# Three small steps of a gate computation moved from VectorE to ScalarE in a streaming encoder kernel

## The chip, the cores and the metric

The kernel runs on one core of one Trainium2 chip. A core has a matrix engine (TensorE, PE in the profile, with its weight loads as PEld), a vector engine (VectorE, DVE), an activation engine (ScalarE, ACT), a third engine for element work (GpSimd, POOL), and an engine that here only issues DMAs (SyncE, SP). Each engine runs its own list of instructions strictly in the order in which the program holds them, and waits at an instruction until the semaphores it needs have been raised by the others. The metric is the device time of one execution, in microseconds; the kernel before took 1362.77 us (median of 3 runs, 1361.56 to 1366.36).

## The reference

One step of an encoder layer over 1024 prompt frames and 32 frames of a running stream. Three groups of heads mix over time in parallel (gated linear attention, HGRN2, mLSTM), and a gated feed-forward network follows. The change lies in the gates of the mixing step:

```python
log_a = log_sigmoid(gg @ gla_w_gate + gla_b_gate) / 16          # first group, tiles 0 and half of 3
log_f = log(lbh + (1 - lbh) * sigmoid(fr))                      # second group, tiles 1, 2, half of 3
k     = (1 - lbh) * sigmoid(-fr)
...
b = cumsum(log_a or log_f)                                      # per block of 64 frames
...
ig = mi + b_i;  log_fm = log_sigmoid(mf + b_f)                  # third group, five rows
w  = exp(b_i - b_j + ig_j - m_i)
```

`lbh` is a lower bound for the gate, one number per channel. `(1 - lbh) * sigmoid(-fr)` can be computed as `exp(log sigmoid(-fr)) * (1 - lbh)`, or as one `exp(log sigmoid(-fr) + log(1 - lbh))`.

## The kernel before, in words

The 1056 frames are taken in three groups (`GROUPS`, L27): 384, 384, and 256 prompt frames with the 32 running ones, 288 columns. For each group `inproj` (L357) computes the normalised input times `w_in`. Every product is a sum of three matmuls (`mm3`, L100: high times high, low times high, high times low), and every weight tile comes in by DMA, is cast on ScalarE or VectorE to its high part and has its low part formed by a subtraction on GpSimd or VectorE (`split`, L105). In group 0 the low parts of the tiles that the gates need are formed on GpSimd and written out, so that groups 1 and 2 load them.

The feature tiles come in a fixed order: 8, 6, 7, 3, 2, 0, 4, 5, 1, 10, 11, 12, 13. In the profile their weights are `wf_8` to `wf_13` and their PSUM results `pf`. All these results, and those of the token tiles (`pv`, weights `wt_1` to `wt_7`), share three PSUM banks of the pool `psb` (tag `big`); TensorE can begin a tile only when the one three places earlier has been read.

Between the tiles stands the work on the gates:

- `decay(f, fill)` (L513), for f = 0 to 3, brings the gate's argument to `fr` and computes `exp(-|fr|)` into `e`, and for f = 1 to 3 the term with the lower bound.
- `rows()` (L564) does the same for the five rows of the third group, on five partitions. `er` is the last of the eight parts of the tile `e`. The exponential at L631 is its first step on ScalarE.
- `logs()` (L524) takes the logarithm of all eight parts in one instruction.
- `decays(f, ins)` (L528) forms the logarithm of the sigmoid (L533), its counterpart for the key (L535), the exponential of that (L536), the product with 1 - lower bound (`oml`, L537), adds the term with the lower bound (L538), divides by 16 where the first group's rows lie (L541, f = 0 and 3; the column of `vecs` holds 1/16 or 1 by partition), and runs the sum over the block (L542). `out_units` writes keys and sums to DRAM by SP.
- `conv(j, ps)` (L374) is a short convolution for tiles 8 and 10 to 13: a copy out of PSUM (L378), a scaled copy (L390), three multiply-adds on VectorE (L392), a tanh (L395, recorded at L113), a last product (L396).

While group g is projected, the mixers of the group before run beside it: `mixer` (L728) is a generator, and `merge` (L1694) advances it a few steps after each tile. A mixer works in three pairs of levels. A pair's scores are matmuls into the one PSUM tile `sc` (L858, a single buffer); VectorE copies them into `P` under a mask (L813, `COPY_PREDICATED`), and the next pair's scores can begin only when the pair before has been copied.

What order the instructions have on each engine is not written out: `schedule_with_timeline_sim` (L81) lets the Tile scheduler place them by its own estimate of their times, within the dependencies, priorities (`high_priority`) and `issue_after` marks of the code. A changed step can so move its neighbours. ScalarE evaluates its functions from a table that is loaded by an own instruction, `ACT_TABLE_LOAD`; the build places one ahead of any function that the loaded table does not hold. The table of the first load serves exponential, tanh, square and copies; the logarithm at L526 has another.

Of the kernel before, what the change touches and what calls it, by code (L numbers as in the profile page):

```python
# [12 lines left out]
AF = mybir.ActivationFunctionType  # L13
ALU = mybir.AluOpType
# [77 lines left out]
def body(ctx: ExitStack, tc: tile.TileContext, a: dict):  # L92
    nc = tc.nc
    act, dve, pool, pe, sp = nc.scalar, nc.vector, nc.gpsimd, nc.tensor, nc.sync
# [62 lines left out]
    def const(name, shape, dt=F32, src=None):  # L157
        t = cp.tile(shape, dt, name=name)
        if src is not None:
            sp.dma_start(t, src)  # L160
        return t
# [10 lines left out]
    vecs = const("vecs_sb", [128, 12], F32, a["vecs"])  # L172
# [41 lines left out]
    dve.tensor_tensor(lb, lsm, lsm, op=ALU.subtract)  # L214
    oml = const("oml", [128, 4])
    dve.tensor_scalar(oml, lb, -1.0, 1.0, op0=ALU.mult, op1=ALU.add)

    def rstd_of(out, ss, n, cols, width, eps=EPS):

        pool.tensor_scalar(out, ss, 1.0 / width, eps, op0=ALU.mult, op1=ALU.add)  # L220
        pool.tensor_tensor(out, out, mhalf[:n, :cols], op=ALU.pow)
# [124 lines left out]
    def out_units(g, dst, dst_s, rng, src, smp_off=None, rows=slice(0, 128), drows=None):  # L346

        t0, pl, sl = GROUPS[g]
        u0, nu = t0 // 128, pl // 128
        drows = rows if drows is None else drows  # L350
        sp.dma_start(dst[(slice(u0, u0 + nu), drows) + rng].rearrange("u p n -> p u n"),
                     src[rows, :pl].rearrange("p (u n) -> p u n", n=128))
        if sl:
            so = pl if smp_off is None else smp_off
            sp.dma_start(dst_s[(drows,) + rng], src[rows, so:so + sl])

    def inproj(g, xh, xl, normed, scaled=None):  # L357
        t0, pl, sl = GROUPS[g]
        T = pl + sl
        R = slice(96, 101)  # L360

        def t1(tag, bufs=1, w=T, dt=F32):
            return pf.tile([128, w], dt, tag=tag, name=f"{tag}_{g}", bufs=bufs)
# [133 lines left out]
        ig = t1("r_ig")  # L497
# [30 lines left out]
        def decays(f, ins):  # L528

            with tc.issue_after(ins.ins):  # L530
                fr, ls = fr4[:, f], e4[:, f]
                lo = (128, 0, 0, 64)[f]
                dve.scalar_tensor_tensor(ls, fr, 0.0, ls, op0=ALU.min, op1=ALU.subtract)  # L533
                if f:
                    dve.tensor_tensor(fr[lo:], ls[lo:], fr[lo:], op=ALU.subtract)  # L535
                    act.activation(fr[lo:], fr[lo:], AF.Exp)  # L536
                    dve.tensor_scalar(fr[lo:], fr[lo:], oml[lo:, f:f + 1], None, op0=ALU.mult)  # L537
                    dve.tensor_tensor(ls, ls, fx4[:, f - 1], op=ALU.add)  # L538
                    out_units(g, qkb_d, qkbs_d, (1, f, slice(None)), fr, None, slice(lo, 128))
                if f in (0, 3):  # L540
                    dve.tensor_scalar(ls, ls, vecs[:, 8 + f:9 + f], None, op0=ALU.mult)  # L541
                dve.tensor_tensor_scan(ls, rmask[:, :T], ls, 0.0, op0=ALU.mult, op1=ALU.add)  # L542
                out_units(g, qkb_d, qkbs_d, (2, f, slice(None)), ls)

# [3 lines left out]
        def store_k(f, k, rows=slice(0, 128)):  # L548
            out_units(g, qkb_d, qkbs_d, (1, f, slice(None)), k, None, rows)
# [14 lines left out]
        def rows():  # L564
# [5 lines left out]
            st = t1("r_st", 1)  # L570
# [6 lines left out]
            for (o, mo, n, c) in segs:  # L577
                dve.tensor_tensor_scan(mr[R, mo + 1:mo + 1 + n], fm[R, o:o + n], ig[R, o:o + n], mr[R, mo:mo + 1],
                                       op0=ALU.add, op1=ALU.max)
# [3 lines left out]
                sp.dma_start(a["q_m"], mr[R, pl + 1 + sl:pl + 2 + sl])  # L583

            dve.tensor_tensor(ig[R], ig[R], bb[R], op=ALU.subtract)
            dve.tensor_copy(st[0:5], ig[R])
            dc = t1("r_dc", 1, 8)
            ci = 0
            for (o, mo, n, c) in segs:
# [62 lines left out]
        store_k(3, kk, slice(0, 64))  # L652
        logs()
        row = rows()
        next(row)
        yield
# [13 lines left out]
        for t, f in ((4, 1), (5, 2)):  # L670
            ps = feat(t)
            q = t1("q", 2)
            ins = silu_q(q, ps, 0)
            store_q(f, q)
            decays(f - 1, ins)
            yield
# [3 lines left out]
        ins = silu_q(q, ps1, 64)  # L680
        store_q(3, q)
        decays(2, ins)
        yield
        for t, j in ((10, 0), (11, 1), (12, 2), (13, 3)):
            ins = conv(j, feat(t))
            if j == 0:
                decays(3, ins)

            next(row, None)
            yield  # L690
# [1267 lines left out]
```

## Time and profile before

| | |
|---|---|
| time, median of 3 runs | 1362.77 us (1361.56 to 1366.36) |
| time of the profiled execution | 1362.2 us |
| its span, from the first instruction to the last | 1360.4 us |
| granted TensorE clock, mean | 0.988 |
| PE busy | 1307.9 us (96%) |
| DVE busy | 1026.7 us (75%) |
| ACT busy | 712.5 us (52%) |
| POOL busy | 320.3 us (24%) |

The three projections fill about the first 500 us of the span, with the mixers of the group before beside the second and third; the last mixers and the output projection reach to about 690 us; the rest is the feed-forward network, which the change does not touch. In the profile a line number is that of the Python source, an operand pair `out<-in` has the buffer numbers left out, and a bracket at the end of a timeline row tells how long the engine stood idle before it and whose instruction ended the wait. Where an instruction waits for several others, the one that came last by the records is named; VectorE runs in order, so a wait for an earlier VectorE instruction can be put down to the one that ends just then.

### The profile page before, as it was taken

What the parts mean: (1) busy time and instruction counts of PE and PEld (TensorE: products, weight loads), DVE (VectorE), ACT (ScalarE), POOL (GpSimd) and SP (SyncE); (2) the same over time, 40 slices, a digit from 0 to 9 for tenths busy, and PEclk for the clock granted to TensorE, in tenths of its full rate; (3) what the DMA queues carried; (4) which work ended last, traced back from release to release, by engine and by line L of the source; (5) the groups of instructions that cost most, each with busy time, mean ns of one, the idle gap of its engine ahead of it and who ended that gap; (6) DMA issues with size and microseconds to landing.
All of it is one profiled execution on the core that took longest, in us unless ns stands there. A gap on an engine that the chain in (4) does not pass through costs nothing.

```text
span 1360.4 us, 29233 instructions
## 1 busy us (share of the span) xinstructions
PE 1307.9 (96%) x11472; PEld 1192.1 (88%) x11472; DVE 1026.7 (75%) x1910; ACT 712.5 (52%) x1374; POOL 320.3 (24%) x529
## 2 busy tenths in 40 slices
PE   6999999998999989999989999999999999999997
PEld 5999989998888977867889999999999996678885
DVE  4786559768598678885798888888888876399566
ACT  4555656554575555444765545545555544444552
POOL 5532403135022154223211112211111110010005
PEclk9999999999998989999999999999999999999999
DMA  9699878886789944544315467546355239654435
GB/s 342 210 326 369 293 261 259 277 280 209 266 252 319 323 146 164 157 149 139 128 48 157 142 146 174 148 116 180 115 152 155 80 132 396 247 161 134 150 104 124
DMA packets 127121, 269.72 MB, mean 198 GB/s; under 512 B 24151, under 2 KB 59639, under 8 KB 126903
## 3 DMA queue, kind: packets, MB, share of 16 engines
q1 hardware_dynamic: 113255, 245.43, 53.0%
q0 software_dynamic: 8928, 18.09, 7.1%
q10 hardware_dynamic: 4800, 4.33, 0.9%
q8 instruction: 90, 1.47, 0.4%
q14 instruction: 48, 0.39, 0.1%
HBM read 206.72 MB, written 86.18 MB: 215 GB/s over the span
## 4 chain that ended last, share of the span: by engine, by line
PE 61%; DVE 8%; ACT 3%; DMA 2%; issue 2%; POOL 1%; SPq 0%; DVEq 0%; POOLq 0%; ACTq 0%
PE pux L102 5%; PE pux L103 5%; PE pux L101 5%; PE puw L101 3%; PE puw L102 3%; PE puw L103 3%; PE q L101 3%; PE q L102 3%; PE q L103 3%; PE x L101 2%; PE x L102 2%; PE x L103 2%; PE puz L101 2%; PE puz L102 2%; PE puz L103 2%
## 5 line engine op out<-in xcount | busy, mean ns | idle before, releaser
L1381 DVE SCALAR_TENSOR_TENSOR y<-uu,fconv_sb,y 128x1060 f32<-128x1060 f32 x88 | 116.1, 1320 | 35.4 <-ACT y L1379 34.9
L1317 ACT COPY c<-pux 128x272 f32<-128x272 f32 (+1 forms) x132 | 49.8, 378 | 47.8 <-PE pux L103 47.1
L101 PE MATMUL pv<-wt_0h,xh 128*128 128x256 f32 (+2 forms) x195 | 57.5, 295 | 3.6 <-DVE xl L322 1.6
L1379 ACT ACTIVATE y<-uu,fconv_sb 128x1060 f32<-128x1060 f32 x44 | 56.1, 1274 | 8.8 <-POOL uu L1375 7.7
L1378 POOL COPY fhalo<-uu 128x2 f32<-128x2 f32 x44 | 16.5, 376 | 185.6 <-DVE uu L1322 185.6
L103 PE MATMUL zp<-woh,cl 128*128 128x512 f32 (+1 forms) x144 | 57.0, 396 | 1.5 <-DVE cl L1088 1.5
L101 PE MATMUL zp<-woh,ch 128*128 128x512 f32 (+1 forms) x144 | 57.0, 405 | 1.2 <-ACT ch L1087 0.8
L102 PE MATMUL zp<-wol,ch 128*128 128x512 f32 (+1 forms) x144 | 57.1, 397 | 0.0
L103 PE MATMUL pv<-wt_0h,xl 128*128 128x256 f32 (+2 forms) x195 | 56.7, 291 | 0.2 <-DVE xl L322 0.2
L103 PE MATMUL pv<-wt_1h,xl 128*128 128x256 f32 (+2 forms) x195 | 56.7, 291 | 0.0
L102 PE MATMUL pv<-wt_0l,xh 128*128 128x256 f32 (+2 forms) x195 | 56.4, 289 | 0.1
L102 PE MATMUL pv<-wt_1l,xh 128*128 128x256 f32 (+2 forms) x195 | 56.3, 289 | 0.0
L101 PE MATMUL pv<-wt_1h,xh 128*128 128x256 f32 (+2 forms) x195 | 56.2, 288 | 0.0
L1557 POOL TENSOR_TENSOR gss<-gss 128x1 f32<-128x1 f32 (+1 forms) x9 | 8.4, 929 | 186.3 <-ACT gjk L1550 186.3
L220 POOL TENSOR_SCALAR hrs<-hss 128x5 f32<-128x5 f32 (+3 forms) x27 | 9.9, 365 | 178.5 <-DVE hss L997 174.6
L813 DVE COPY_PREDICATED P<-masks_sb,sc 128x352 f32<-128x352 int32 (+3 forms) x53 | 37.7, 712 | 6.3 <-PE sc L726 5.8
L101 PEld LDWEIGHTS pv<-wt_0h,xh 128*128 128x128 f32 (+1 forms) x195 | 37.3, 191 | 5.5 <-ACT xh L321 2.2
L103 PEld LDWEIGHTS pv<-wt_0h,xl 128*128 128x128 f32 (+1 forms) x195 | 37.3, 191 | 0.6 <-DVE xl L322 0.4
L102 PEld LDWEIGHTS pv<-wt_0l,xh 128*128 128x128 f32 (+1 forms) x195 | 37.2, 191 | 0.6 <-POOL wt_0l L110 0.5
L101 PEld LDWEIGHTS pv<-wt_1h,xh 128*128 128x128 f32 (+1 forms) x195 | 37.4, 192 | 0.4 <-issue 0.2
L103 PEld LDWEIGHTS pv<-wt_1h,xl 128*128 128x128 f32 (+1 forms) x195 | 37.0, 190 | 0.5 <-issue 0.2
L102 PEld LDWEIGHTS pv<-wt_1l,xh 128*128 128x128 f32 (+1 forms) x195 | 37.2, 191 | 0.1
(1716 smaller groups left out, 5304.1 us busy)
## 6 DMA issues: line engine op xcount, KB each, us to landing
wrP<-in_w_dn SPq DMA_DIRECT2D x27, 512.0 KB, 3.7
h_d<-y SPq DMA_DIRECT2D x22, 530.0 KB, 3.3
ht<-h_d SPq DMA_DIRECT2D x22, 530.0 KB, 9.4
wt_0r<-in_w_tok SPq DMA_DIRECT2D x21, 512.0 KB, 5.5
wt_1r<-in_w_tok SPq DMA_DIRECT2D x21, 512.0 KB, 6.2
ws_d<-in_w_dn POOLq DMA_DIRECT2D x20, 512.0 KB, 9.2
wrP<-ws_d SPq DMA_DIRECT2D x20, 512.0 KB, 4.5
wt_0l<-lt_d SPq DMA_DIRECT2D x14, 512.0 KB, 7.6
```

Of the source, the lines that this page charges most:

```text
L101: pe.matmul(ps, lh[0], rh[0], start=first, stop=False, **kw)
L102: pe.matmul(ps, lh[0], rh[1], start=False, stop=False, **kw)
L103: return pe.matmul(ps, lh[1], rh[0], start=False, stop=last, **kw)
L220: pool.tensor_scalar(out, ss, 1.0 / width, eps, op0=ALU.mult, op1=ALU.add)
L813: dve.copy_predicated(dst, mk.broadcast_to([n, 11, *mk.shape[2:]]), src)
L1317: kept[name] = act.copy(t, ps)
L1378: behind["POOL"] = pool.tensor_copy(fhalo[:, j, :], u[:, NCOL - 2:NCOL])
L1379: act.activation(y, u, AF.Identity, scale=fconv[:, j, 2:3], bias=fconv[:, j, 3:4])
L1381: dve.scalar_tensor_tensor(y, uu[i][:, s:s + NCOL], fconv[:, j, s:s + 1], y, op0=ALU.mult, op1=ALU.add)
L1557: pool.tensor_tensor(ss[:n, 0:1], ss[:n, 2:3], ss[:n, 3:4], op=ALU.add)
```

## The change

Four places, all in the gate computation:

- A new constant `lom`, the logarithm of `oml`, is computed once at the start on ScalarE.
- In `decays`, the product with `oml` on VectorE (L537) is dropped, and the exponential at L536 gets `lom` as its bias. Three instructions per group, nine in all, leave VectorE.
- In `decays`, the scaled copy at L541 (f = 0 and f = 3, two per group, six in all) moves from VectorE to ScalarE.
- In `rows`, the copy of the five gate rows into `st` (L586, one per group, three in all) moves from VectorE to ScalarE.

```diff
@@ constants
     dve.tensor_scalar(oml, lb, -1.0, 1.0, op0=ALU.mult, op1=ALU.add)
+    lom = const("lom", [128, 4])
+    act.activation(lom, oml, AF.Ln)
@@ decays
                     dve.tensor_tensor(fr[lo:], ls[lo:], fr[lo:], op=ALU.subtract)
-                    act.activation(fr[lo:], fr[lo:], AF.Exp)
-                    dve.tensor_scalar(fr[lo:], fr[lo:], oml[lo:, f:f + 1], None, op0=ALU.mult)
+                    act.activation(fr[lo:], fr[lo:], AF.Exp, bias=lom[lo:, f:f + 1])
                     dve.tensor_tensor(ls, ls, fx4[:, f - 1], op=ALU.add)
...
                 if f in (0, 3):
-                    dve.tensor_scalar(ls, ls, vecs[:, 8 + f:9 + f], None, op0=ALU.mult)
+                    act.activation(ls, ls, AF.Copy, scale=vecs[:, 8 + f:9 + f])
                 dve.tensor_tensor_scan(ls, rmask[:, :T], ls, 0.0, op0=ALU.mult, op1=ALU.add)
@@ rows
             dve.tensor_tensor(ig[R], ig[R], bb[R], op=ALU.subtract)
-            dve.tensor_copy(st[0:5], ig[R])
+            act.copy(st[0:5], ig[R])
```

In the changed file the lines behind the new constant are numbered two higher than before, and from `decays`' dropped line on one higher (L631 becomes L632).

What moves on the engines, at three places. First ScalarE in group 0, early in the program: `L561` writes the argument of the first gate, `L631` is the first exponential of the five rows, `L390` and the cast of `wf_3` follow. Before:

```order
L561 ACTIVATE fr_391<-z_0_394,vecs_sb 128x384
L631 ACTIVATE e_392<-e_392 5x384
L390 ACTIVATE y_381<-pc_377,mconv_sb 128x384
L107 CAST wf_3h<-wf_3r 128x1024
L518 ACTIVATE e_392<-e_392 128x384
```

And now:

```order
L562 ACTIVATE fr_393<-z_0_396,vecs_sb 128x384
L632 ACT_TABLE_LOAD
L632 ACTIVATE e_394<-e_394 5x384
L392 ACTIVATE y_383<-pc_379,mconv_sb 128x384
L107 CAST wf_3h<-wf_3r 128x1024
L520 ACTIVATE e_394<-e_394 128x384
```

The logarithm for `lom` stands earlier on ScalarE with a table load of its own, so the exponential here has a load ahead of it that was not there. After both the list goes on as before: the loads at the logarithm of each group, and after it, are the same in number.

Second, ScalarE at the end of the gates of group 0, among the convolutions of tiles 10 to 13 (`pc` are copies out of their PSUM tiles). Before:

```order
L378 COPY pc_887<-pf_12_862 128x384
L536 ACTIVATE fr_391<-fr_391 64x384
L390 ACTIVATE y_891<-pc_887,mconv_sb 128x384
L113 ACTIVATE th_851<-y_846 128x384
L107 CAST wt_2_1h<-wt_2_1r 128x1024
L378 COPY pc_932<-pf_13_907 128x384
```

And now:

```order
L380 COPY pc_886<-pf_12_861 128x384
L538 ACTIVATE fr_393<-fr_393,lom 64x384
L542 ACTIVATE e_394<-e_394,vecs_sb 128x384
L392 ACTIVATE y_890<-pc_886,mconv_sb 128x384
L113 ACTIVATE th_850<-y_845 128x384
L107 CAST wt_2_1h<-wt_2_1r 128x1024
L380 COPY pc_931<-pf_13_906 128x384
```

The moved copy stands between the exponential and the convolution's scaled copy; the copy that frees the PSUM bank of tile 13 is one further back.

Third, TensorE in group 2, where a mixer's third pair of scores (`sc_4`) stands among the projection of the token tile `pv_1_0`. Before:

```order
L101 MATMUL pv_1_0_5774<-xh_4317,wt_1_1h 128x288
L102 MATMUL pv_1_0_5774<-xl_4318,wt_1_1h 128x288
L103 MATMUL pv_1_0_5774<-xh_4317,wt_1_1l 128x288
L101 MATMUL pv_1_0_5774<-xh_4317,wt_1_1h 128x288
L102 MATMUL pv_1_0_5774<-xl_4318,wt_1_1h 128x288
L726 MATMUL sc_4_5629<-Qz_152,Ld_150 64x2x32
```

And now:

```order
L103 MATMUL pv_1_0_5767<-xh_4313,wt_1_0l 128x288
L101 MATMUL pv_1_0_5767<-xh_4313,wt_1_0h 128x288
L102 MATMUL pv_1_0_5767<-xl_4314,wt_1_0h 128x288
L103 MATMUL pv_1_0_5767<-xh_4313,wt_1_0l 128x288
L101 MATMUL pv_1_0_5767<-xh_4313,wt_1_0h 128x288
L727 MATMUL sc_4_5622<-Qz_154,Ld_152 64x2x32
```

Ten projection matmuls that stood ahead of the scores now stand behind them. In the same way nine matmuls of tile 12 now stand behind the second pair of scores, four of tile 5 behind the memory products `oi`, and seventeen of `pv_1_1` behind the products `og` that close the mixer. On VectorE in group 2 the six dropped instructions are gone and the neighbours keep nearly their order. Outside groups 0 to 2 one place changes, the first product of the down projection, at about 1165 us of the span: there the scheduler takes the casts of its operands in a slightly different order.

## The prediction

> **What bounds the kernel now.** I read the busy shares first, then the idle times of TensorE with what ended them, then the granted clock around the longest of them, and last the lists of the other engines backwards from each.
>
> ```profile
> span 1360.4 us, 29233 instructions
> PE 1307.9 (96%) x11472; PEld 1192.1 (88%) x11472; DVE 1026.7 (75%) x1910; ACT 712.5 (52%) x1374; POOL 320.3 (24%) x529
> ```
>
> TensorE is the bound: it is idle for 1360.4 - 1307.9 = 52.5 us, and the change neither adds nor takes matmuls. So it can only alter some of those idle times, or open new ones. These are the ones near the changed steps, by the timeline of TensorE (start, duration, and in brackets the idle time ahead with its releaser):
>
> ```profile
> 62.03 0.44 PE L101 MATMUL pf<-xh,wf_5h 128*128 128x384 f32 x1 [1.36 <-ACT q L661]
> 72.79 0.45 PE L101 MATMUL pf<-xh,wf_10h 128*128 128x384 f32 x1 [1.93 <-DVE q L556]
> 97.27 0.39 PE L101 MATMUL pv<-wt_0h,xh 128*128 128x256 f32 x1 [0.41 <-ACT pc L378]
> 228.01 0.44 PE L101 MATMUL pf<-xh,wf_11h 128*128 128x384 f32 x1 [0.75 <-DVE q L556]
> 418.62 1.14 PE L726 MATMUL sc<-Qz,Ld 64*64 64x64 f32 x64 [2.09 <-DVE e L541]
> 447.21 0.40 PE L101 MATMUL pv<-xh,wt_0h 128*128 128x288 f32 x1 [0.95 <-ACT vf L475]
> ```
>
> Together they are 7.5 us, 0.55% of the time. Idle time can cost more than its length, as the table of windows around two of them shows (length, busy time of PE, PEld, DVE, ACT and POOL, granted clock, DMA share, GB/s):
>
> ```profile
> core 0: us, PE busy (x) PEld busy (x) DVE busy (x) ACT busy (x) POOL busy (x), PEclk, DMA share, GB/s
> 376.00:424.00 48.00, 44.00 (x544) 41.15 (x543) 45.77 (x118) 33.28 (x76) 13.11 (x23) 0.96 0.84 268
> 418.00:420.00 2.00, 1.38 (x67) 1.37 (x67) 2.00 (x5) 0.24 (x2) 0.39 (x2) 1.00 1.08 389
> 422.00:424.00 2.00, 2.00 (x27) 1.60 (x25) 1.43 (x5) 0.45 (x1) 0.00 (x0) 0.50 0.70 208
> 424.00:426.00 2.00, 2.00 (x10) 2.00 (x10) 1.93 (x4) 0.40 (x1) 0.00 (x0) 0.50 0.86 252
> 71.00:75.00 4.00, 2.21 (x12) 2.21 (x13) 2.78 (x3) 1.48 (x3) 2.37 (x1) 1.00 0.94 266
> ```
>
> After the 2.09 us at 418.62 the clock falls to 0.50; after the 1.93 us at 72.79 it stays at 1.00. Whether a stall of about 2 us brings a slow stretch is thus not decided by its length alone. And from 376 to 424 VectorE is busy for 45.77 of 48 us: in group 2, and there only, VectorE bounds the work beside the projection.
>
> **The change part by part.** The prices, by line (minimum, median and maximum in ns):
>
> ```profile
> L537 DVE TENSOR_SCALAR fr<-fr,oml x9: 341/420/421, 79.8 to 415.0; 128x384 f32<-128x384 f32 x4, 64x384 f32<-64x384 f32 x2, 128x288 f32<-128x288 f32 x2, 64x288 f32<-64x288 f32 x1
> L541 DVE TENSOR_SCALAR e<-e,vecs_sb x6: 345/412/419, 74.7 to 418.3; 128x384 f32<-128x384 f32 x4, 128x288 f32<-128x288 f32 x2
> L586 DVE COPY r_st<-r_ig x3: 351/352/1014, 67.9 to 386.2; 5x384 f32<-5x384 f32 x2, 5x288 f32<-5x288 f32 x1
> L667 ACT ACTIVATE q<-pf x3: 410/484/493, 65.8 to 384.6; 128x384 f32<-128x384 f32 x2, 128x288 f32<-128x288 f32 x1
> L820 ACT ACTIVATE qe<-q,cf_sb x36: 306/387/404, 139.9 to 553.5; 128x128 f32<-128x128 f32 x32, 128x32 f32<-128x32 f32 x4
> ```
>
> VectorE loses 18 instructions, 9 x 0.42 + 6 x 0.41 + 2 x 0.35 + 1.01 = about 8 us. ScalarE gains nine: a scaled copy like L667 takes 0.49 us at 384 columns (L820, scaled by a column as the new one is, takes 0.39 at 128 columns, so a little more is possible; I take 0.5), a copy of five rows about as much. The bias at L536 changes no count. With two table loads ScalarE gets about 7 us more. Shares of 75% and 52% say nothing about the time; each place has to be followed.
>
> *The table loads.* Both ends of the first part of group 0, on the engines that pass the work on:
>
> ```profile
> 16.45 0.59 ACT L321 CAST xh<-xt 128x512 fp32r<-128x512 f32 x1 [1.22 <-PE xt L318]
> 19.96 0.18 ACT L443 COPY tgs<-pv 128x26 f32<-128x26 f32 x1 [2.93 <-PE pv L103]
> 36.33 1.03 ACT L107 CAST wf_3h<-wf_3r 128x1024 fp32r<-128x1024 f32 x1
> 37.44 2.56 POOL L110 TENSOR_TENSOR wf_3l<-wf_3r,wf_3h 128x1024 fp32r<-128x1024 f32 x1 [2.65 <-ACT wf_3h L107]
> 36.45 3.95 DVE L392 SCALAR_TENSOR_TENSOR y<-pc,mconv_sb,y 128x384 f32<-128x384 f32 x3 [0.72 <-ACT y L390]
> 40.33 0.68 DVE L109 CAST wf_2h<-wf_2r 128x1024 fp32r<-128x1024 f32 x1
> 53.22 2.59 POOL L110 TENSOR_TENSOR wf_5l<-wf_5r,wf_5h 128x1024 fp32r<-128x1024 f32 x1 [0.68 <-DVE wf_5h L109]
> 56.06 0.53 ACT L521 ACTIVATE e<-e 128x384 f32<-128x384 f32 x1 [1.95 <-DVE e L520]
> 56.61 1.28 ACT L526 ACT_TABLE_LOAD   x1
> 57.90 2.77 ACT L526 ACTIVATE e<-e 128x3072 f32<-128x3072 f32 x1
> 61.51 0.47 ACT L661 COPY q<-pf 128x384 f32<-128x384 f32 x1
> ```
>
> A load takes 1.28 us. The first, with the logarithm of `lom` (0.2 us), comes between 17.0 and 19.96, where ScalarE idles for 2.93 us: it costs nothing, and there are 1.4 us of cover left. The second stands where ScalarE has no gap. It puts the cast of `wf_3` 1.28 us later, and from there the work goes hand to hand: GpSimd forms `wf_3l` behind that cast, VectorE's third convolution step ends only when GpSimd is through (3.95 us for three steps, to 40.40, against GpSimd's end at 40.00), then VectorE casts `wf_2`, GpSimd forms its low part, and so on to `wf_5l` at 53.22, behind which L520 and L521 come, the logarithm, and at 61.51 the copy that frees the PSUM bank for which TensorE waits at 62.03. I find no idle time on this way that isn't itself a wait for the step ahead, so the whole load arrives: +1.3 us (bounds 0 and, should it shift a DMA too, +1.6).
>
> By the Trainium skill's page "ScalarE: Activation LUTs", section "What ACT_TABLE_LOAD costs", a switch is 1283 ns and about 1380 ns of drain, 2.66 us in all; the sum would then be 1.4 us higher. The trace shows the first figure and not the second: L521 ends at 56.59, the load follows at 56.61, the logarithm at 57.90.
>
> *The copy of the gate rows.* L586 stands on the chain that ends in the wait at 72.79:
>
> ```profile
> 67.91 0.35 DVE L586 COPY r_st<-r_ig 5x384 f32<-5x384 f32 x1
> 71.66 0.48 ACT L113 ACTIVATE th<-pf 128x384 f32<-128x384 f32 x1
> ```
>
> Behind it on VectorE follow L593 and L598, for which ScalarE waits; then come a cast and the tanh at 71.66, then VectorE's L556, then TensorE. On ScalarE the copy goes into a gap ahead of L599. Gain: -0.35.
>
> *The scaled copies.* For f = 1 and 2 there are none. In group 0, for f = 3, the copy now stands in ScalarE's list ahead of work that was ready:
>
> ```profile
> 94.26 0.55 DVE L538 TENSOR_TENSOR e<-e 128x384 f32<-128x384 f32 x1
> 94.27 0.71 ACT L390 ACTIVATE y<-pc,mconv_sb 128x384 f32<-128x384 f32 x1
> 95.38 0.53 ACT L113 ACTIVATE th<-y 128x384 f32<-128x384 f32 x1 [0.39 <-DVE y L392]
> ```
>
> It must wait for L538's end at 94.81 and takes 0.5 us, so L390 begins at about 95.4 in place of 94.27, 1.1 later; the idle 0.39 ahead of the tanh takes up a part, and +0.7 is left for the cast and the copy L378 behind it, which frees the bank that TensorE awaits at 97.27. It was already late by 0.41 there, so +0.7 (bounds 0 and +1.1). For f = 0 the copy stands ahead of a cast that was waiting for a DMA: nothing. In groups 1 and 2 TensorE does not wait behind these copies.
>
> *Group 1.* The wait at 228.01 is for L556 on a busy VectorE, ahead of which now an L541 and an L537 are gone:
>
> ```profile
> 225.27 0.42 DVE L537 TENSOR_SCALAR fr<-fr,oml 128x384 f32<-128x384 f32 x1
> 227.39 0.56 DVE L556 SCALAR_TENSOR_TENSOR q<-th,pf 64x384 f32<-64x384 f32 x1
> ```
>
> Each frees about 0.33 us (0.42 less what neighbours overlap): -0.65 of the 0.75.
>
> *Group 2.* The wait at 418.62 carries the name of L541, which ends at that moment, but the scores use a single PSUM tile and need the last masked copy of the pair before:
>
> ```profile
> 417.54 0.93 DVE L813 COPY_PREDICATED P<-masks_sb,sc 128x352 f32<-128x352 int32 x1
> 413.70 0.29 PE L101 MATMUL pv<-xh,wt_0h 128*128 128x288 f32 x1
> 413.83 0.29 PE L102 MATMUL pv<-xl,wt_0h 128*128 128x288 f32 x1
> ```
>
> Of VectorE's list ahead of that copy go L586 (1.01), one L541 and three L537 (0.34 to 0.37 each, less overlap): 2.3 us in all, so the copy and the scores come 2.3 us earlier. But the scheduler has counted on that: ten projection matmuls, 0.14 us apart, now stand behind the scores, so TensorE arrives earlier too and still waits for about 2 us. What is gained is 2.3 - 10 x 0.14 = -0.9. At 447.21 the copy of `vf` now stands ahead of an exponential that waited for VectorE; between 0 and -0.95 I take -0.5.
>
> The changed order at the down projection I leave at zero.
>
> Sum: +1.3 - 0.35 + 0.7 - 0.65 - 0.9 - 0.5 = -0.4 us. The profiled execution took 1362.2 us, so 1361.8; the median of the runs lies 0.6 above it, so I forecast 1362.4, no change (within 0.3%, 4.1 us, about what a measurement of this kernel tells from none).
>
> **The rivals.**
>
> *ScalarE blocks at the moved copies (slower).* A scaled copy waits for VectorE, and every cast and every copy out of PSUM behind it waits with it. The price is at most the 1.1 us worked out for f = 3, at six places: 6.6, with the load 7.9, and if VectorE's relief is worth nothing 1362.8 + 7.9 = 1370.7. It passes 4.1 us when three of the six places cost all of it beside the load. For it speaks 97.27; against it that ScalarE is busy for 33.28 of 48 us in group 2. Chance 0.15.
>
> *A new slow stretch of the clock at 62.* The wait there grows to 1.36 + 1.28 = 2.64 us, longer than the one that was followed by clock 0.50. A mean clock of 0.96 over the 48 us to 424 and 0.50 over the 2 us behind them are 1.9 + 1.0 = 2.9 us lost; a stretch half as long costs 1.5. This gives 1363.9 to 1365.3, above 0.3% only with other losses. Against it: 1.93 us at 72.79 left the clock alone. Chance 0.18.
>
> *The slow stretch in group 2 goes (faster).* If the scores meet a shorter wait, or it falls differently, the 2.9 us are gained, with some of the wait, about 1.2: 1358.3. Against it: the ten matmuls moved keep the wait at about 2 us. Chance 0.17.
>
> The Trainium skill's page "TensorE: Matmul & The Clock Gate", section "HAM oscillation — how this bites in real kernels", has the gate close on idle gaps above about 3.4 us. By that rule neither clock rival exists and the forecast stands; the 0.50 after a gap of 2.09 us speaks against it.
>
> **How the numbers follow.** Forecast 0.46, the three rivals 0.15, 0.18 and 0.17, and 0.04 for a change that leaves no trace. Within 0.3%: 0.46 + 0.04 + two thirds of the 0.18 = 0.62; slower: 0.15 + 0.06 = 0.21; faster 0.17. The range runs from the faster rival, 1357.5, to 1368.5, between the clock rival and the worst of the blocking; about 1 in 10 is left out at each end.
>
> **What the profile would show.** Right: a load ahead of the first exponential of the five rows at about 35 us and TensorE's wait for L661 near 2.6 us; the wait for tile 10 near 1.6; the one for L378 above 1; the one in group 1 nearly gone; the third scores in group 2 about 2 us earlier against their surroundings, with a wait still ahead of them. Wrong, if the wait for L661 is as before (a gap absorbed the load), if the clock shows 0.50 in a stretch where it was 1.00 or the reverse, or if the sums of TensorE's waits agree and the time does not.

## The result and the profile after

The changed kernel took 1370.46 us (median of 15 executions, 1366.85 to 1373.28), the kernel before 1366.36 us (median of 15, 1361.56 to 1370.70). The ratio is 1.0033, with a 95% interval of 1.0022 to 1.0045: slower by about 4.5 us. The forecast was 1362.4 us and no change. Of the 8.1 us between forecast and median, 3.6 are its base: the three executions shown before had a median of 1362.77, fifteen have 1366.36. The other 4.5 lie in the sum, and that is what the experiments are about.

The page of the changed kernel's profiled execution (1372.92 us) has these busy shares:

```profile
span 1371.1 us, 29222 instructions
PE 1315.4 (96%) x11472; PEld 1198.2 (87%) x11472; DVE 1020.9 (74%) x1892; ACT 721.1 (53%) x1386; POOL 319.4 (23%) x529
```

VectorE lost 5.8 us of work and ScalarE gained 8.6 (about 8 and 7 were forecast); TensorE's idle time went from 52.5 to 1371.1 - 1315.4 = 55.7 us. The timeline of TensorE has these waits where the prediction looked, and where new ones stand (start, duration, idle time ahead and its releaser):

```profile
63.40 0.69 PE L101 MATMUL pf<-xh,wf_5h 128*128 128x384 f32 x1 [2.46 <-ACT q L662]
84.78 0.44 PE L101 MATMUL pf<-xh,wf_12h 128*128 128x384 f32 x1 [1.05 <-DVE q L557]
100.04 0.39 PE L101 MATMUL pv<-wt_0h,xh 128*128 128x256 f32 x1 [0.85 <-ACT pc L380]
150.08 0.32 PE L727 MATMUL sc<-Qz,Ld 64*64 64x64 f32 x4 [1.25 <-DVE Qz L848]
249.81 0.44 PE L727 MATMUL mi<-ident,kh 128*128 128x128 f32 x2 [0.84 <-ACT kt L875]
420.66 1.13 PE L727 MATMUL sc<-Qz,Ld 64*64 64x64 f32 x64 [1.03 <-DVE P L814]
428.28 0.92 PE L727 MATMUL og<-v,P 64*64 64x64 f32 x24 [1.20 <-DVE P L814]
482.87 1.27 PE L727 MATMUL om<-vm,w 64*64 64x65 f32 x20 [4.00 <-DVE cat L1000]
486.31 0.58 PE L101 MATMUL pv<-xh,wt_0h 128*128 128x288 f32 x1 [0.83 <-DVE gth L430]
```

The waits of 1.93 us at tile 10, of 0.75 us in group 1 and of 0.95 us for `vf` in group 2 are gone. In their place are waits that were not there (84.78, 150.08, 249.81, 428.28) and one of 4.00 us for `cat`, the normalised output of the mixers, at 482.87. The same place in the kernel before:

```profile
477.76 0.80 PE L726 MATMUL om<-vm,w 64*64 64x65 f32 x20 [1.21 <-DVE cat L999]
479.02 0.80 PE L726 MATMUL oi<-C,mqz 128*64 128x65 f32 x20 [0.45 <-DVE cat L999]
481.19 0.37 PE L101 MATMUL pv<-xh,wt_0h 128*128 128x288 f32 x1 [1.37 <-DVE gth L428]
```

Comparing the start of the same work in both traces tells where the time was lost: the changed kernel is 1.4 us late at 62 us, 2.8 at 97, 2.8 at 228, 3.8 at 353 (the first matmul of group 2's tile 8, 352.56 to 356.31), then 2.0 at the third scores of group 2 (418.62 to 420.66) and 2.3 at 458, and 5.1 at 478 (477.76 to 482.87). So the gain in group 2 came (1.4 us by 458), and 2.8 us were lost within 20 us of 458.

**What TensorE waits for at 482.87.** The norm's product writes `cat` on VectorE. Ahead of it in VectorE's list stands a step of another unit: the decay of the state S of the unit with the stream's frames, S being loaded from memory by a DMA. The issue of that DMA on SP, and the two steps on VectorE; first before:

```profile
470.28 0.33 SPq L770 DMA_DIRECT2D S<-in_s_gh  x1
...
476.73 0.42 DVE L910 TENSOR_TENSOR S<-S,dec 128x256 f32<-128x256 f32 x1 [3.57 <-DMA S<-in_s_gh]
477.07 0.55 DVE L999 TENSOR_TENSOR cat<-og,hrs 128x384 f32<-128x384 f32 x1
```

and after:

```profile
473.61 0.38 SPq L771 DMA_DIRECT2D S<-in_s_gh  x1
...
481.83 0.43 DVE L911 TENSOR_TENSOR S<-S,dec 128x256 f32<-128x256 f32 x1 [6.36 <-DMA S<-in_s_gh]
482.17 0.55 DVE L1000 TENSOR_TENSOR cat<-og,hrs 128x384 f32<-128x384 f32 x1
```

The load of 128 KB landed 6.45 us after its issue before and 8.22 us after it now, and was issued 3.3 us later. It shares the 16 DMA engines with weight blocks of 512 KB; the share of DMA time was 0.82 before and is 0.93 now in the table of windows:

```profile
470.00:478.00 8.00, 6.79 (x79) 6.39 (x74) 4.04 (x18) 2.21 (x9) 3.63 (x5) 1.00 0.82 291
```

```profile
470.00:478.00 8.00, 8.00 (x140) 7.74 (x136) 2.77 (x13) 2.40 (x8) 3.33 (x4) 1.00 0.93 337
```

**The clock.** Behind the waits at 63.40 and 482.87 the granted clock is 0.50. Windows of 3.41 us in the changed kernel (columns as in the prediction's table: length, busy time of PE, PEld, DVE, ACT and POOL, clock, DMA share, GB/s):

```profile
59.77:63.18 3.41, 1.17 (x7) 0.85 (x5) 1.07 (x2) 3.41 (x3) 0.13 (x1) 1.00 0.50 166
63.18:66.59 3.41, 3.19 (x10) 3.19 (x11) 3.41 (x2) 2.40 (x3) 3.41 (x2) 0.50 0.20 60
66.59:70.01 3.42, 3.42 (x21) 3.42 (x20) 3.32 (x5) 1.52 (x3) 2.21 (x1) 1.00 0.00 0
...
336.26:339.67 3.41, 1.77 (x34) 1.49 (x25) 3.41 (x11) 3.40 (x8) 0.68 (x2) 1.00 0.87 188
339.67:343.08 3.41, 3.41 (x18) 3.40 (x17) 3.41 (x12) 1.71 (x6) 2.22 (x2) 0.50 0.51 207
...
479.61:483.02 3.41, 0.15 (x5) 0.18 (x7) 1.19 (x4) 0.01 (x1) 0.22 (x1) 1.00 0.85 286
483.02:486.43 3.41, 2.58 (x41) 2.27 (x39) 3.38 (x12) 2.38 (x7) 3.05 (x5) 0.50 0.08 22
486.43:489.85 3.42, 3.42 (x15) 3.42 (x16) 3.21 (x9) 1.73 (x5) 2.38 (x4) 0.50 0.32 114
489.85:493.26 3.41, 3.41 (x42) 3.13 (x42) 1.28 (x5) 1.71 (x5) 0.69 (x2) 1.00 0.22 54
```

Every slow stretch of both traces is one such window or several, and all of one trace begin on one grid of 3.413 us; in the changed kernel's trace from 63.18 to 339.67 are 81.0 steps, from there to 483.02 another 42.0. One window at 0.50 is up to 1.71 us lost. The changed kernel's profiled execution has twelve of them, that of before eight ahead of its last matmul. So of the 10.7 us between the two profiled spans up to 4 x 1.71 = 6.8 are windows, and some of these (at 647, 688, 695 us) stand in a part of the program where the waits are much the same in both traces. That may be chance: the mean granted clock was 0.9855 over the 15 executions of the changed kernel and 0.9839 over 35 of the kernel before. The two profiles lie at opposite ends of their kernels' executions, and only the waits ahead of the windows are used below.

By the Trainium skill, page "TensorE: Matmul & The Clock Gate", section "What's actually happening", the activity window is free-running and 3413 ns long; the trace agrees, with 3.41 us and a grid. The Trainium skill's section that the prediction weighed has the gate close on gaps above about 3.4 us; the trace disagrees, with 0.50 behind a gap of 2.46 us.

### The profile page after: what moved, and what is told of

Read it like the earlier page. It is cut to its first block, busy times and chain, and to the rows that moved or that the text cites. A ratio compares the mean times of both kernels' runs of the same rounds, so it can differ in the third digit from the quotient of the medians.

```text
span 1371.1 us, 29222 instructions
## 1 busy us (share of the span) xinstructions
PE 1315.4 (96%) x11472; PEld 1198.2 (87%) x11472; DVE 1020.9 (74%) x1892; ACT 721.1 (53%) x1386; POOL 319.4 (23%) x529
## 3 DMA queue, kind: packets, MB, share of 16 engines
q1 hardware_dynamic: 113255, 245.43, 52.5%
## 4 chain that ended last, share of the span: by engine, by line
PE 59%; DVE 9%; DMA 3%; ACT 3%; issue 2%; POOL 1%; SPq 0%; ACTq 0%; DVEq 0%; POOLq 0%
PE pux L102 5%; PE pux L103 5%; PE pux L101 4%; PE puw L103 3%; PE puw L102 3%; PE puw L101 3%; PE q L101 3%; PE q L102 3%; PE q L103 3%; PE x L101 2%; PE x L102 2%; PE x L103 2%; PE puz L101 2%; PE puz L103 2%; PE puz L102 2%
## 5 line engine op out<-in xcount | busy, mean ns | idle before, releaser
L223 POOL TENSOR_TENSOR hrs<-hrs,mhalf 128x5 f32<-128x5 f32 (+3 forms) x27 | 36.5, 1352 | 2.2
```

## The experiments

The ratios below are to the kernel before on the same chip, with 95% intervals; 0.1% is 1.37 us. Kernels that stand in one group were compared with the same executions of the kernel before (medians from 1365.0 to 1365.6 us).

### One part at a time, and the full change without the loads

The bias alone:

```diff
+    lom = const("lom", [128, 4])
+    act.activation(lom, oml, AF.Ln)
...
-                    act.activation(fr[lo:], fr[lo:], AF.Exp)
-                    dve.tensor_scalar(fr[lo:], fr[lo:], oml[lo:, f:f + 1], None, op0=ALU.mult)
+                    act.activation(fr[lo:], fr[lo:], AF.Exp, bias=lom[lo:, f:f + 1])
```

> Only the decays' part of the change: the logarithm of 1 - lower bound is a bias of the exponential, and the nine products on VectorE are gone; both ScalarE copies are back on VectorE. Theory A (the two added loads of the activation table cause the loss): the wait of TensorE for L661 or L662 at about 62 us grows from 1.36 to 2.4 us or more, the work at 97 us comes 1.5 to 3 us late, and the whole is 2 to 5 us slower than before, as the full change is. Rival B (ScalarE blocks at the moved copies): this kernel is within 1 us of before. Rival C (group 2 gives back what VectorE gains, through transfers that land late): the wait for cat at about 480 us is 2.5 us or more here too.

Measured: 1369.09 us, ratio 1.0028 (1.0008 to 1.0048). The wait at 62 us is 2.43 us, with a window at 0.50 behind it; but the work at 97 us is only 0.9 us late, since the next wait (tile 10) fell from 1.93 to 0.59 us. The wait for `cat` is 2.66 us. So A is right on the wait and wrong on what is left of it at 97 us, and C is right as well: this kernel is level with the one before at 458 us and 1.4 us late at 478.

The scaled copies alone, and the copy of the five rows alone:

```diff
-                    dve.tensor_scalar(ls, ls, vecs[:, 8 + f:9 + f], None, op0=ALU.mult)
+                    act.activation(ls, ls, AF.Copy, scale=vecs[:, 8 + f:9 + f])
```

```diff
-            dve.tensor_copy(st[0:5], ig[R])
+            act.copy(st[0:5], ig[R])
```

> Only the six products for the divisor (L541 of before) move to ScalarE. Theory A (table loads): nothing is lost here, 0 to 1 us slower, from the wait for L378 at 97 us alone. Rival B (blocking at the moved copies): 2 to 4 us slower, with longer waits of TensorE behind the copies in groups 0 and 1. Rival C (group 2): the wait at about 418 us shrinks by 0.4 us and the waits at about 478 us take it back.

> Only the copy of the gates' five rows (L586 of before) moves to ScalarE. Theory A: 0 to 0.4 us faster (the wait for tile 10 at 72.8 us falls from 1.93 to 1.6 us; in group 2 VectorE is relieved of 1.0 us). Rival B: up to 1 us slower. Rival C: whatever is gained by 420 us is gone by 480 us.

Measured: the scaled copies 1369.69 us, 1.0028 (1.0011 to 1.0046); the copy of the rows 1367.60 us, 1.0016 (0.9999 to 1.0033). The theory that the loads are all of it is thus out: two kernels without any added load are slower, one of them plainly. In the first, TensorE is not held at L378; `cat` is waited for 2.31 us. In the second the forecast wait is there and so is what it opened; TensorE's timeline:

```profile
72.17 0.44 PE L101 MATMUL pf<-xh,wf_10h 128*128 128x384 f32 x1 [1.55 <-DVE q L556]
...
83.61 0.45 PE L101 MATMUL pf<-xh,wf_12h 128*128 128x384 f32 x1 [0.97 <-DVE q L556]
```

The 0.38 us won at tile 10 are spent two tiles later (0.97), and the work at 97 us is 1.3 us late. C does not hold for this kernel: it is 1.4 us early at 478 us, and TensorE does not wait for `cat` ahead of `om` there.

The full change, with the logarithm behind that of group 0, whose table is loaded anyway:

```diff
             with tc.high_priority(offset=LNA):
-                act.activation(e8, e8, AF.Ln, bias=1.0)
+                ins = act.activation(e8, e8, AF.Ln, bias=1.0)
+                if g == 0:
+                    with tc.issue_after(ins.ins):
+                        act.activation(lom, oml, AF.Ln)
```

> The full change, but the logarithm of 1 - lower bound is taken right behind the logarithm of group 0, whose table is loaded then anyway, so that no table load is added (8 in place of 10). Theory A: the wait at 62 us is back at 1.4 us, the clock stays at 1.00 behind it, the work at 97 us is no more than 0.7 us late, and the whole is 2.5 to 3 us below the full change, +1 to +2 us against before. Rivals B and C: the loads are not the cause, and the whole stays 3 to 5 us above before.

Measured: 1367.12 us, 1.0021 (1.0003 to 1.0039). The wait at 62 us is 1.55, the clock behind it stays at 1.00, the work at 97 us is 1.1 us late, and at 458 us this kernel is 1.9 us early. At 478 us nothing of it is left: the wait for `cat` is 3.03 us. The whole is 0.12% (1.6 us) below the full change, less than the interval and less than the 2.5 to 3 us that A expected.

### The loads alone, and the state S

The kernel before with `lom` computed at the start and used by nothing:

> The kernel before, with the logarithm of 1 - lower bound computed at the start and used by nothing: two table loads are added, no product and no copy is moved. Theory A (the loads make the loss of the first 100 us): the wait for L661 or L662 at 62 us is 2.4 to 2.7 us, and the work at 97 us is 1.3 us late, or 2.5 to 3 us where the grid of the clock's windows falls as in the full change; the whole is 1 to 3 us slower than before. Rival (the order made around the change, not the loads): the wait at 62 us stays below 1.7 us, and the whole is within 1 us of before.

Measured: 1368.01 us, 1.0025 (1.0008 to 1.0043). The wait is the full change's:

```profile
63.20 0.44 PE L101 MATMUL pf<-xh,wf_5h 128*128 128x384 f32 x1 [2.47 <-ACT q L663]
```

A window at 0.50 follows, and 1.2 us are left at 97 us and at 458 us. The whole is 3.4 us slower, but its interval begins at 1.1, so it isn't shown that more was lost than those 1.2 us. The tile of `lom`, which this kernel has too, is looked at below.

The full change, the kernel before, and the full change with the late logarithm, each with the load of S near the start of the program (at 13 us), to a tile of its own:

```diff
+        if u == 5:
+            S = mx.tile([128, 4, 64], F32, tag="S8", name="S8", bufs=1)
+            sp.dma_start(S, a["s_gh"])
+            state["S", True] = S
...
-                sp.dma_start(S, a["s_gh"])
                 sp.dma_start(C, a["s_c"])
```

> The full change, and the load of the decode unit's state S (128 KB) is issued near the start of the program, to a tile of its own, in place of behind the weight blocks at 473.6 us. Theory D (VectorE stands at the decay of S until the load lands, and the norm's product behind it on VectorE holds TensorE): the wait of 4.00 us for cat at 482.9 us falls to 1.5 us or less, one or both of the slow windows of the clock behind it go, and the whole is 2.5 to 5 us faster than the full change: 0 to +2 us against before. Rival E (something else holds the norm's product or TensorE at that place, the transfers behind it above all): the wait stays above 3 us or moves by 10 us, and the whole is within 1 us of the full change, +3.5 to +5.5 us against before.

> The kernel before with the load of S near the start, as in the run of the full change beside it. Theory D: the wait of 1.21 us for cat at 477.8 us goes, with one slow window of the clock in some executions: 1 to 3 us faster than before. Rival E: within 1 us of before.

> The full change with both repairs: the logarithm behind that of group 0, so that no table load is added, and S loaded near the start. If loads (A) and state (D) are the two causes and the relief of VectorE in group 2 is worth what stood at 457 us in the run with the late logarithm (1.9 us early), this is 1 to 3 us faster than before. If group 2's gain is given back whatever lands early (E), it is +1 to +3 us against before, as the late logarithm alone.

Measured: 1363.47 us, 0.9999 (0.9983 to 1.0016); 1365.64 us, 1.0004 (0.9987 to 1.0021); 1363.23 us, 0.9988 (0.9973 to 1.0004). In all three the wait for `cat` is gone. The full change falls by 0.34% and is level with the kernel before, as D said; with the late logarithm it is 0.12% below, which the interval doesn't tell from none. The kernel before gained nothing, against D: the load at 13 us stands among the first weights, and the wait at 62 us grew from 1.36 to 2.29 us with a window at 0.50 behind it (3.33 and 2.39 us in the other two). At 478 us its profile has a wait of 2.16 us for `vf` in place of those for `cat` and `gth`, and two more slow windows near 600 us. The load at this place also changes the order of other work on all four computing engines, from about 22 us on, so these three kernels show more than the load.

### S in group 1, and the 16 bytes of `lom`

In the feed-forward part, where TensorE doesn't wait, the changed kernel takes longer for the same matmuls. The same stretch of it in the kernel before, and in the changed kernel:

```profile
704.38:1049.50 345.12, 345.12 (x2849) 345.12 (x2847) 287.04 (x477) 178.52 (x306) 60.61 (x160) 1.00 0.53 146
```

```profile
713.02:1059.77 346.75, 346.75 (x2849) 346.75 (x2848) 287.42 (x477) 178.55 (x307) 61.42 (x159) 1.00 0.53 146
```

This 0.47% can come from the place of the tiles behind `lom` in the on-chip memory (SBUF), which its 16 bytes per partition move. To see that, one kernel is the one before with an unused tile of that size, and one is the full change with `lom` written over a tile that is read no more:

```diff
+    pad = const("pad", [128, 4])
```

```diff
-    lom = const("lom", [128, 4])
+    lom = lmx
     act.activation(lom, oml, AF.Ln)
```

> The kernel before with one more tile of 128 x 4 numbers (16 bytes per partition) beside oml that nothing writes or reads: every engine's list is the same as before, only the places of the tiles behind it in SBUF move by 16 bytes. Theory F (lom's 16 bytes move the operands of the feed-forward part, and the matmuls read them a little slower): TensorE takes 346.75 us for the stretch of 2848 matmuls that takes 345.12 before, and the whole is 1.6 to 2 us slower than before. Rival G (the other pace comes from the table loads, the clock or the state of the chip): the stretch takes 345.12 us and the whole is as before.

> The full change, with lom written over lmx, a part of a tile that is read no more, so that no tile is added; every engine's list is that of the full change. Theory F: the stretch takes 345.1 us in place of 346.75, and the whole is 1.6 to 2 us below the full change, +2.5 to +3 us against before. Rival G: the stretch stays at 346.75 us and the whole at +4.5 us.

The stretch follows the place to the hundredth: it takes 346.75 us in all eight kernels with `lom` or the unused tile as an added tile, and 345.11 in all twelve without. With the unused tile, and with `lom` in place:

```profile
706.37:1053.12 346.75, 346.75 (x2849) 346.75 (x2848) 287.32 (x477) 178.34 (x306) 60.34 (x160) 1.00 0.52 145
```

```profile
712.99:1058.10 345.11, 345.11 (x2848) 345.11 (x2847) 287.15 (x477) 178.59 (x308) 61.33 (x160) 1.00 0.53 146
```

In the whole it can't be seen: with the unused tile 1365.26 us, 1.0004 (0.9985 to 1.0022), where 1.6 to 2 us (0.12 to 0.15%) were expected, which the interval doesn't exclude; with `lom` in place 1368.33 us, 1.0019 (1.0005 to 1.0033), 0.14% below the full change, as expected but no more than the interval. So F holds for the stretch, and its worth for the whole is not shown. In the executions with the unused tile the mean granted clock was 0.0016 higher (about 2.2 us), which could pay for it; why is open.

The load of S behind the gate load of unit 3 in group 1 (issued at 348 us):

```diff
         ins = sp.dma_start(gt[:n], g_d[t0:t0 + n, :])
+        if u == 3:
+            with tc.issue_after(ins.ins):
+                S = mx.tile([128, 4, 64], F32, tag="S8", name="S8", bufs=1)
+                sp.dma_start(S, a["s_gh"])
+                state["S", True] = S
...
-                sp.dma_start(S, a["s_gh"])
                 sp.dma_start(C, a["s_c"])
```

> The kernel before, with the load of S issued behind the gate load of unit 3, in group 1, in place of near the start; the rest of the order stays. Theory D: the wait of 1.21 us for cat at 478 us goes and nothing is lost at 62 us (the load near the start cost 0.9 us there, 2.29 in place of 1.36): 1 to 3 us faster than before. Rival H (the time won there is waited for at the next late thing, as when the load stood near the start, where the whole was as before): within 1 us of before.

> The full change with three repairs: the logarithm behind that of group 0 (no table load added), lom in place (no tile added), S loaded in group 1. If loads, place in SBUF and state are the whole loss and VectorE's relief is worth 1 to 2 us: 2 to 4 us faster than before, below both kernels. If the relief is given back elsewhere: within 1 us of before.

Measured: the kernel before with S there 1360.59 us, 0.9961 (0.9948 to 0.9974), which is 5.3 us and more than D's 1 to 3; the full change with all three repairs 1358.67 us, 0.9957 (0.9942 to 0.9972), 5.9 us where 2 to 4 were expected. Both beat the kernel before, and they can't be told apart. With the load here, in this kernel and in those below, the order on the four computing engines is that of the same kernel with S behind the weights, but for two neighbours on VectorE at about 358 us and at most two on TensorE at about 500; so these pairs show the load itself.

### What is left of the change with S out of the way

The full change, the scaled copies alone and the copy of the rows alone, each with S in group 1, and the repaired change with S where it was:

> The full change with the load of S in group 1, as in the kernel before with S there; the order is else that of the full change. If S holds most of the loss (D): the wait for cat at 482.9 us (4.00) goes, and the whole is 5 to 8 us below the full change, 0 to 3 us below before; what stays above the kernel before with S in group 1 (0.9961) is the loads and the slow window at 63 us, 2 to 3 us. If the loads and copies hold most (A, B): 2 us or less below the full change, +2 to +4 us against before.

> The scaled copies alone on ScalarE, with the load of S in group 1. If their price is S's late landing (D): within 1 us of the kernel before with S in group 1 (0.9961), 4 to 6 us below before. If ScalarE blocks at them (B): 2 us or more above that kernel, 2 to 3 us below before.

> The copy of the five rows alone on ScalarE, with the load of S in group 1. If what group 2 gains arrives once S is out of the way (D): 0 to 2 us below the kernel before with S in group 1, 0.995 to 0.996 of before. If the copy costs something of its own in the early groups (B, the new wait for tile 12 at 83.6 us, 0.97 us): 1 to 2 us above it.

> The full change without added table loads and without an added tile, S loaded as before. It differs from all_repairs by the load of S alone. D: 4 to 6 us above all_repairs, 0 to +1 us against before. If S is worth no more than its wait of 3 us in the run with the late logarithm: 2 to 3 us above all_repairs, 3 to 4 us below before.

Measured, beside the same kernels with S behind the weights:

```
                                         S behind the weights     S in group 1              difference
kernel before                            1                        0.9961 (.9948 to .9974)   0.39%
full change                              1.0033 (1.0022 to 1.0045) 0.9975 (.9958 to .9991)  0.58%
full change, no loads, no added tile     1.0009 (.9988 to 1.0030) 0.9957 (.9942 to .9972)   0.52%
scaled copies alone                      1.0028 (1.0011 to 1.0046) 0.9987 (.9974 to .9999)  0.41%
copy of the rows alone                   1.0016 (.9999 to 1.0033) 0.9963 (.9951 to .9975)   0.53%
```

Two windows of TensorE around that place, the full change with S behind the weights and with S in group 1 (the same work lies 2.3 us earlier there ahead of the wait, 6.4 behind it):

```profile
478.00:490.00 12.00, 7.17 (x63) 6.66 (x62) 7.93 (x22) 4.11 (x11) 5.65 (x8) 0.72 0.50 158
```

```profile
474.00:486.00 12.00, 11.78 (x132) 11.06 (x130) 9.63 (x25) 5.92 (x16) 8.33 (x12) 1.00 0.65 207
```

TensorE is busy for 11.78 of 12 us in place of 7.17, at full clock in place of 0.72. The load of S costs the full change 0.58% (7.9 us) and the kernel before 0.39% (5.3 us). Taken by these medians 2.6 us more are lost there with the change, near the 2.8 us of longer wait in the trace; the other 0.14% (1.9 us) of its 0.33% stay with S out of the way, and are gone (0.9957 against 0.9961) when the loads and the added tile go too. But each of these differences has an interval of about 0.2%. What is shown is that the load costs every one of the five kernels 0.4 to 0.6%, and that the three repairs together take away the change's loss: 0.33% above the kernel before without them, level with it (S in group 1 in both) with them. How the 0.33% divide between S and the rest is not shown by the totals. The scaled copies alone are 0.26% above their reference even with S in group 1, against D.

Whether the scaled copies cost that in the repaired change as well, two last kernels ask: it without the scaled copies, and without both copies.

> The full change with the three repairs, without the scaled copies (L541 of before stays on VectorE). If the parts add up, as scale_S_mid against before_S_mid says (0.26%): 3 to 4 us below all_repairs, 0.993 of before. If the scaled copies cost only where the order around them is that of the kernel before: within 1.5 us of all_repairs, 0.995 to 0.997.

> The bias alone with the three repairs (late logarithm, no added tile, S in group 1); both copies stay on VectorE. If the nine products that VectorE loses are worth something once nothing else is in their way: 1 to 3 us below the kernel before with S in group 1, 0.994 to 0.9955 of before. If not: 0.996 to 0.997.

Measured: 1358.35 us, 0.9953 (0.9939 to 0.9968), and 1358.09 us, 0.9947 (0.9933 to 0.9962). Against 0.9957 with both copies this is no difference that can be told, so the 0.26% of the scaled copies are shown for the kernel before only; an interval of about 0.2% doesn't exclude a like cost in the repaired change. The traces give a hint where it arises: in six of the ten kernels with the scaled copies TensorE waits 1.0 to 1.6 us for `Qz` at about 150 us, and in four 0.6 to 1.0 us for `kt` at about 249, and in none of the ten kernels without them is there either wait. How the copies bring this about is not settled. The bias alone with the three repairs has the lowest median of all kernels; it is 0.53% below the kernel before, of which 0.39% are S, and the rest is within the interval.

## Why the prediction was wrong

**The step that failed** is the end of the sum, the last of group 2 and the sentence on the changed order. The sum booked -0.9 and -0.5 us as final where VectorE was relieved, and put nothing for what is late next on VectorE's list. The relief came, 1.4 us from 353 to 458 us. What is late next was the decay of S, which waited for a DMA in the kernel before too (3.57 us, in a row that the prediction didn't show), with the product for TensorE behind it. A faster VectorE didn't make the transfer land earlier: with the late logarithm TensorE was 1.9 us early at 458 us, S landed 0.1 us earlier than before, and the wait for `cat` grew from 1.21 to 3.03. In the full change S landed 5.1 us later. Why the load took 8.22 us there and 6.45 before is shown only as a fuller DMA queue. In that place 2.8 us of wait were added and a second window at 0.50.

The size differs between executions: with `lom` in place, where every engine's order is that of the full change, the same wait is 1.97 us and not 4.00. The sign held in these traces. Of the ten kernels with the load behind the weights, the six in which the bias or the scaled copies moved wait 1.97 to 4.00 us for `cat` and have two windows at 0.50 behind it; the other four wait at most 1.21 and have one window or none.

**The sum was off ahead of that place too.** It had the work 1.65 us late at 97 us and 1.0 behind group 1; the profile has 2.8 and 3.8. At 97 us 1.4 of it is the slow window that the prediction held as a rival; behind that come two waits that it didn't have, for `Qz` (1.25) and for `kt` (0.84). And the 16 bytes of `lom`, put at nothing, lengthen the feed-forward stretch by 1.6 us. The three repairs (loads, tile, S) together take the loss away; the share of each of these terms in the 4.5 us stays open.

Point by point:

- *First table load: hidden.* Right; it runs at 16.64 us in the gap named.
- *Second load: +1.3.* Right in size (+1.1): 1.36 to 2.46 us, 2.47 with the loads alone, 1.55 without them. What the sum missed is that the next wait takes most of it back (tile 10: 1.93 to 0.48 us with the loads alone), and that the slow clock spends it again.
- *The clock rival at 62 us (0.18).* It happened. In all eight kernels where this wait was 2.29 us or more a window at 0.50 followed; in none of the twelve with 1.55 or less. Its price of 1.5 was near the 1.71 of a window. It was given too small a chance because 1.93 us at 72.79 had left the clock alone in one trace. That was luck: in three of the six kernels with 1.90 to 1.93 us there a slow window followed. What differs is where the wait lies on the grid. In the kernel before the edge of a window parts it, and TensorE is busy for 1.96 us of the first window; with the scaled copies alone it lies in one window, with 1.51 us busy:

```profile
68.90:72.31 3.41, 1.96 (x12) 1.65 (x10) 1.21 (x4) 2.58 (x5) 0.47 (x1) 1.00 0.68 114
72.31:75.72 3.41, 2.93 (x17) 2.93 (x17) 3.34 (x4) 1.05 (x2) 1.90 (x1) 1.00 0.95 357
...
70.55:73.96 3.41, 1.51 (x9) 1.19 (x8) 1.53 (x2) 1.82 (x3) 1.88 (x1) 1.00 0.97 197
73.96:77.37 3.41, 3.41 (x13) 3.41 (x12) 2.36 (x4) 1.94 (x3) 1.33 (x2) 0.50 1.02 391
```

Over all twenty traces, of the windows at full clock that begin between 58 and 75 us, where nearly all matmuls fill the array, each of the eleven with TensorE busy for 1.52 us or less was followed by 0.50, and none with 1.57 or more.

- *Copy of the rows: -0.35.* Right at tile 10 (-0.38), wrong as a sum: +1.3 at 97 us, most of it through a wait for tile 12 (0.97) that the kernel before doesn't have.
- *Scaled copy at f = 3: +0.7 at L378.* Right in place, too large in size: the wait there grew from 0.41 to 0.85. It is 0.80 to 0.91 in eight of the ten kernels with the scaled copies and at most 0.50 in the ten without. In the other two, the scaled copies alone with either load of S, there is none; there a slow window at 74 us had already made TensorE late.
- *Group 1: -0.65.* The wait at 228 us went; a new one of 1.25 us for `Qz` at 150 us took its place, and the work at 228 us is as late as at 97. The wait for `kt` at 249.81 comes on top.
- *Third scores: -0.9 with a wait still near 2 us.* The scores are 2.0 us late where group 2 began 3.8 late, and the wait fell to 1.03; but ten matmuls (1.4 us) now stand behind them. By 458 us 1.4 us are left of it all, what -0.9 and -0.5 made together. That the sum fits is in part luck: the slow windows at 420 to 427 went as well, which was the faster rival, and its 2.9 us did not show, a new wait of 1.20 us for the masked copies being one reason. Nor did they go for good: every other kernel, that with `lom` in place among them, has one or two slow windows that begin between 408 and 428 us.
- *Blocked ScalarE (0.15).* Not shown. The scaled copies alone cost 0.28%, but no such cost is seen in the repaired change. The new waits for `Qz` and `kt` come only where these copies moved; that ScalarE stands at a copy until VectorE is through was not found to be their cause.

The range reached to 1368.5 and the median was 1370.46; from a base of 1366.36 in place of 1362.77 the same sum would have missed by 4.5 us as well.

## What to carry to other kernels

Before a stall is booked as won, look at what the relieved engine does next in its list, and whether any of it waits for a DMA: a load that lands at its own time takes the gain back, and everything behind it in that list waits too. An order made by a scheduler moves other work with every edit, so single parts need not add up to the whole; compare them at fixed places of the trace, not by their totals alone. And a wait of TensorE of 2 us can cost 2 us or nearly 4, by where it falls on the clock's grid, so one execution doesn't tell which.

## What was not expected of the hardware

- In these traces the granted clock changes only on a grid of 3.413 us, and long idle time isn't needed for it. In the window of the changed kernel ahead of the slow one at 510.33, TensorE is idle for 0.15 us only; 60 of its 64 matmuls there are on parts of the array, 32 x 32 to 128 x 32 (`mi`, `og`, `sc` and `sm` of the unit with 32 frames). That this is why the clock fell was not tried:

```profile
506.91:510.33 3.42, 3.27 (x64) 2.45 (x62) 3.33 (x13) 1.80 (x5) 2.10 (x4) 1.00 0.57 153
510.33:513.74 3.41, 3.41 (x26) 2.59 (x24) 3.22 (x9) 2.76 (x3) 1.65 (x3) 0.50 1.12 318
```

- An unused tile of 16 bytes changed the pace of TensorE in a stretch without any wait from 345.12 to 346.75 us (0.47%), at a granted clock of 1.00, and taking it away changed it back. What in the new places costs that wasn't tried.
- One load of 128 KB, issued behind weight blocks, cost the kernel before 0.39%, 5.3 us (3.6 to 7.1): more than the 3.0 us of idle time behind it (1.21, 0.45 and 1.37). The slow window that follows adds up to 1.7.
